# Recurrent layer of a two-layer decoder step: one visit per head with the 32-column products of three heads, states 32 projection steps behind it

## The chip, the cores and the metric

The kernel runs on one core of one Trainium2 chip, as one launch. The metric is device time in microseconds (us), median of three runs. One further execution was profiled; its trace gives each instruction's engine, start and duration. Engines: PE (TensorE matmuls), PEld (TensorE weight loads), DVE (VectorE), ACT (ScalarE), POOL (GpSimd) and SP (SyncE, which issues most DMAs).

## The reference

One inference step for 320 tokens: 256 prompt tokens, and 8 sequences with 8 new tokens each that share the weights; 16 learned meta tokens lead the prompt, so 336 columns pass through layer 0. Width 2048. Layer 0 is a gated linear recurrence (HGRN2, 16 heads of 128), layer 1 is sliding-window attention; each layer has one input projection, a gate, one output projection and a layer norm behind the residual sum. The change touches layer 0 only.

```python
def hgrn_chunk(q, logf, k, v, s0):
    b = jnp.cumsum(logf, axis=1)                       # products of the forget gates
    diff = jnp.where(causal, b[:, :, None] - b[:, None, :], -jnp.inf)
    a = jnp.sum(q[:, :, None] * jnp.exp(diff) * k[:, None, :], axis=-1)
    o = (jnp.einsum('bthk,bhkv->bthv', q * jnp.exp(b), s0)
         + jnp.einsum('btsh,bshv->bthv', a, v))
    s_new = (jnp.exp(b[:, -1])[..., None] * s0
             + jnp.einsum('bshk,bshv->bhkv', k * jnp.exp(b[:, -1][:, None] - b), v))
    return o, s_new

def hgrn_branch(xin, w_in, lb, norm_w, w_out, s0, n_lead, chunk):
    q, fx, i_in, g = jnp.split(jnp.einsum('btd,de->bte', xin, w_in), 4, axis=-1)
    f = lb + (1.0 - lb) * jax.nn.sigmoid(heads(fx))
    q, logf, k, v = heads(q), jnp.log(f), 1.0 - f, heads(i_in)
    ...                                                # chunks one after the other, state carried on
    o = o * lax.rsqrt(jnp.mean(jnp.square(o), axis=-1, keepdims=True) + RMS_EPS) * norm_w
    o = o.reshape(bsz, t, HGRN_WIDTH) * jax.nn.silu(g)
    return jnp.einsum('bte,ed->btd', o, w_out), s
```

Outputs are the tokens and the new recurrent states: one state of 128 x 128 per head for the prompt (`st_p`) and eight for the samples (`st_s`).

## The kernel before

**The stream.** All projections are one stream on TensorE. For each head there are four weight tiles of 128 output columns, in the order f (forget), q, i (values), g (gate); each takes 16 steps of k. A step of k is three matmuls of 128 x 336 (L225 to L227): the weight and the input are each split in a high and a low part, low times high, high times low and high times high. Weights come as `raw` by DMA (L148, SP), four k at a time; ACT casts the high part `whi` (L159) and DVE subtracts for the low part `wlo` (L170), seven chunks ahead of use. The chunk with the last four k of a tile is taken first, so a tile starts with its `wlo_..._3`. Behind each step the stream lets side generators emit some of a head's own work; `yield n` in such a generator means "n steps later". The order of emission is the order of the queues: each engine takes its instructions strictly in that order.

**A head's own work.** `head_chain(h)` builds the products over time by doubling: levels of 1, 2, 4 and 8 tokens give `lv_a`, products with 32 output columns (L514); VectorE picks from them by mask (L521, L522). Levels of 16 to 64 give `lv_b` (L514, L591, L596). kx and qx are the scaled keys and queries of a level. Then follow the transposes `pk`, `pv` (L603, L606), the state products `psp` (prompt, L660) and `pss` (samples, L664), the output `po` (32-column products L692 to L699, then 128-column ones L701 to L704), its squares on ACT (L709), the mean `ss` (L710, DVE), its power on POOL (L711), the scaling `osc` (L714, DVE), the transposes `pt` (L720) and the gated output `og`, `oh`, `ol` (L725, L278, L279), which is the input of the output projection. `ns` is the samples' new state: s0 times fs on POOL (L675), plus pss on DVE (L679), stored by SP (L680).

**Where it stands.** Two visits per head interrupt the projections. Visit a, four steps into tile g of head h: lv_a of head h, psp and pss of h-1, pt of h-2. Visit b, 14 steps later, in tile f of the next head: lv_b, pk and pv of head h, po of h-1. PSUM buffers are few: `pj` and `pm` banks rotate between projections and head products, `lv` holds lv_a and lv_b, and pt is written into the old lv_b.

**The end of the layer.** The output projection has 16 tiles z0 to z15. Three of them (z0 to z2) run side by side, k outermost, while the last heads finish, since each k of theirs needs one head's output. From z3 on they go one after the other. A `z_chain` behind each tile adds the residual (L790, L791), scales (L792, L793 and L794), and writes the next layer's input xh (L795) and xl (L804). The z buffers are opened in memory that the recurrence's pool has given back, so z0 waits until the last ns has been stored.

Of the kernel before, what the change touches and what calls it, by code (L numbers as in the profile page):

```python
# [21 lines left out]
F32 = mybir.dt.float32  # L22
# [217 lines left out]
def hybrid_trunk(tc, x_prompt, x_sample, state_hgrn, cache_k, cache_v, meta, w_in0, lb_logits, norm_w, w_out0,  # L240
# [7 lines left out]
    with es:  # L248
# [97 lines left out]
        for nm, w in (("f", 384), ("qp", 448), ("iT", 384), ("at", 3 * 132), ("a32", 96), ("sq0", 288),  # L346
                      ("sq1", 288), ("qi0", 177), ("qi1", 177), ("w64", 72)):
            one[nm] = hp1.tile([P, w], F32, tag=nm, name=nm)
            nc.gpsimd.memset(one[nm], 1.0 if nm == "w64" else 0.0)
        kx, qx = [], []  # L350
        for q in range(1, 4):
            for l, nm, w in ((kx, "kx", 384), (qx, "qx", 448)):
                l.append(hp1.tile([P, w], F32, tag=f"{nm}{q}", name=f"{nm}{q}"))
                nc.gpsimd.memset(l[-1], 0.0)
# [90 lines left out]
        def epi_g(h):  # L445
            def epi(ps):
                d = head_state(h)
                sg = hp.tile([P, T], F32, tag="sg", name=f"sg{h}")
# [3 lines left out]
                nc.sync.dma_start(s0, state_hgrn[0, :, h].rearrange("b k v -> k b v"))  # L452
                d["s0"] = s0

                def chain():
                    yield 2
                    nc.vector.tensor_tensor(sg, sg, ps, op=ALU.mult)  # L457
                    ready["g", h] = True
                st.spawn(chain())
            return epi  # L460
# [5 lines left out]
        def update(k, q, m, tot, n, k2=None, q2=None, nq=None):  # L466
# [5 lines left out]
            w = min(n, 448 - (m - 1)) // (2 * m) * 2 * m  # L472
# [4 lines left out]
            if q2 is not None and not nq:  # L477
                nc.scalar.copy(halves(q2, m - 1, m, w, True), halves(q, m - 1, m, w, True))
# [17 lines left out]
        tails = {}  # L496

        def adv(h):
            if h in tails:
                next(tails[h], None)  # L500

        def head_chain(h):
            d = head_state(h)
            kr, qp, a32, sq, qi = d["kr"], d["qp"], d["a32"], d["sq"], d["qi"]
            at = d["at"].rearrange("p (b w) -> p b w", b=3)
            kk = [kr] + kx
            qq = [qp] + qx

            def level(pl, o, li, wide=True):
                k, q = kk[min(li, 3)], qq[min(li, 3)]  # L510
                for blk in range(3):
                    for j in range(4 if blk < 2 else 3 if wide else 1):
                        c = blk * 128 + j * 32
                        nc.tensor.matmul(pl[32 * j:32 * j + 32, o + blk * 32:o + blk * 32 + 32], k[:, c:c + 32],  # L514
                                         q[:, c:c + 32], start=True, stop=True, tile_position=(0, 32 * j),
                                         skip_group_check=True)

            def pick(pl, o, li, wide=True):
                m0 = li * 96
                r = 96 if wide else 32  # L520
                nc.vector.copy_predicated(a32[:, 0:64], mk[:, m0:m0 + 64], pl[:, o:o + 64])  # L521
                nc.vector.copy_predicated(a32[0:r, 64:96], mk[0:r, m0 + 64:m0 + 96], pl[0:r, o + 64:o + 96])  # L522

            tot = {1: d["f"]}
            yield 3
            for li in range(3):
                m = 1 << li
                update(kk[li], qq[li], m, tot[m], 352, kk[li + 1], qq[li + 1])
                tot[2 * m] = total(h, m, tot[m], 352)
                yield 4  # L530

            k8, q8 = kk[3], qq[3]
            fs = hp.tile([P, 8], F32, tag="fs", name=f"fs{h}")
            t8 = tot[8]
            nc.gpsimd.tensor_copy(fs, t8[:, 36:44])
            w64 = d["w64"]
            nc.gpsimd.tensor_copy(w64[:, 0:64].rearrange("p (b t) -> p b t", t=8)[:, :, 7], fs)

            for s in range(3):
                n = 3 if s < 2 else 2  # L540
                nc.gpsimd.tensor_tensor(sq[:, 0:96 * n].rearrange("p (j w) -> p j w", w=96)[:, :, 40 * s:40 * s + 8],
                                        q8[:, 288:288 + 24 * n].rearrange("p (j w) -> p j w", w=24)[:, :, 8 * s:8 * s + 8],
                                        w64[:, 0:24 * n].rearrange("p (j w) -> p j w", w=24)[:, :, 8 * s:8 * s + 8],
                                        op=ALU.mult)
            yield 4

            pa = lv.tile([P, 512], F32, tag="lv", name=f"lv{h}_a")
            for li in range(4):
                level(pa, 96 * li, li)
            adv(h - 1)  # L550
            adv(h - 2)
            yield 1
            update(k8, q8, 8, t8, 272)
            tot[16] = hp.tile([P, 17], F32, tag="tot16", name=f"tot{h}_16")
            t8v = t8[:, 0:34].rearrange("p (b two) -> p b two", two=2)
            nc.vector.tensor_tensor(tot[16], t8v[:, :, 0], t8v[:, :, 1], op=ALU.mult)
            for li in range(4):
                pick(pa, 96 * li, li)
            adv(h - 1)
            yield 2  # L560
            t16 = tot[16][:, 16:17]
            update(k8, q8, 16, tot[16], 256, kk[1], qq[1])
            tot[32] = total(h, 16, tot[16], 256)
            nc.vector.tensor_scalar(qq[1][:, 271:272], q8[:, 271:272], t16, None, op0=ALU.mult)
            yield 3
            adv(h - 2)
            update(kk[1], qq[1], 32, tot[32], 256, kk[2], qq[2])
            nc.scalar.copy(qi[:, 144:161], qq[1][:, 255:272])
            t64 = total(h, 32, tot[32], 256)
            t128 = hp.tile([P, 2], F32, tag="t128", name=f"t128_{h}")  # L570
            nc.vector.tensor_tensor(t128[:, 0:1], t64[:, 2:3], t64[:, 3:4], op=ALU.mult)
            yield 3
            adv(h - 1)
            k64 = kk[2]
            nc.vector.tensor_tensor(halves(kr, 0, 64, 256), halves(k64, 0, 64, 256),
                                    t64.rearrange("p (b two) -> p b two", two=2)[:, :, 1:2].to_broadcast([P, 2, 64]),
                                    op=ALU.mult)
            nc.scalar.copy(halves(kr, 0, 64, 256, True), halves(k64, 0, 64, 256, True))
            nc.vector.tensor_scalar(qi[:, 64:128], qq[2][:, 191:255], t64[:, 2:3], None, op0=ALU.mult)
            nc.scalar.copy(qi[:, 0:64], qq[2][:, 127:191])  # L580
            yield 5
            while ("i", h) not in ready:
                yield 0

            pb = lv.tile([P, 512], F32, tag="lv", name=f"lv{h}_b")
            d["pb"] = pb
            level(pb, 0, 4, wide=False)
# [11 lines left out]
            adv(h - 1)  # L599
            iT = d["iT"]  # L600
            pk = pm(f"pk{h}")
            for j in range(3):
                nc.tensor.transpose(pk[:, j * P:(j + 1) * P], (kr if j < 2 else k8)[:, j * P:(j + 1) * P], ident)  # L603
            pv = pm(f"pv{h}")
            for j in range(3):
                nc.tensor.transpose(pv[:, j * P:(j + 1) * P], iT[:, j * P:(j + 1) * P], ident)  # L606
            yield 1
            pick(pb, 0, 4, wide=False)
            for a in range(2):
                nc.scalar.copy(at[64 * a:64 * a + 32, 0:2, 64 * a + 32:64 * a + 64],  # L610
                               pb[64 * a:64 * a + 32, 96:160].rearrange("p (b w) -> p b w", b=2))
            nc.scalar.copy(at[0:64, 0:2, 64:128], pb[0:64, 160:288].rearrange("p (b w) -> p b w", b=2))
            for blk in range(3):
                o = 1 if blk < 2 else 0
                nc.vector.copy_predicated(
                    at[:, blk, o:o + 128].rearrange("p (j w) -> p j w", w=32),
                    mk[:, 480 + blk * 128:608 + blk * 128].rearrange("p (j w) -> p j w", w=32),
                    a32[:, blk * 32:blk * 32 + 32].unsqueeze(1).to_broadcast([P, 4, 32]))
            V = hp1.tile([P, 3, P], F32, tag="V", name=f"V{h}")
            K = hp1.tile([P, 2, P], F32, tag="K", name=f"K{h}")  # L620
# [27 lines left out]
            for w, us in ((1, (h - 1,)), (3, (h - 1,)), (6, (h,)), (2, (h - 1, h)), (1, (h - 1, h)), (4, (h,)), (3, (h,)),  # L648
                          (2, (h,)), (4, (h,)), (1, (h,))):
                yield w  # L650
                for u in us:
                    adv(u)
# [849 lines left out]
```

## Time and profile before

| | |
|---|---|
| time, median of 3 runs | 1155.39 us (1155.0 to 1156.29) |
| time of the profiled execution | 1155.55 us |
| its span, first to last instruction | 1153.5 us |
| mean granted TensorE clock | 0.997 |
| PE / DVE / ACT / POOL busy | 1138.6 / 795.3 / 619.8 / 238.8 us |
| DMA traffic | 173.39 MB, mean 150 GB/s |
| TensorE's longest waits | 1.2 us (pj_z for DVE sg), 1.1, 1.0, 0.7, 0.6 |

A row of a timeline gives the start, the duration, the engine, line and operation, the output and inputs, the count, and in brackets the idle time ahead of it with what ended it. Matmul durations overlap, so costs on PE are differences of starts. A product of plain f32 counts as two matmuls in the trace and as one in the order lists below.

### The profile page before, as it was taken

To read this page: it belongs to the slowest core of one execution; us is meant where nothing else is said; L and a number is where in the kernel's file an instruction comes from. 1 tells how busy PE (TensorE), PEld (TensorE's weight loads), DVE (VectorE), ACT (ScalarE), POOL (GpSimd) and SP (SyncE) were. 2 spreads that over 40 slices of the span, in tenths; PEclk is the share of its full clock that TensorE was granted. 3 is DMA by queue.
4 is the path that set the end of the run, shared out by engine and by line. 5 is a ranking of instruction groups with operands and counts; after the bars stand their busy time and mean duration, and the time that the engine had idled before them with its cause. 6 is when DMAs were issued, how large, how long until landed. Compare 5 with 4: busy or idle time off the path is not lost.

```text
span 1153.5 us, 26363 instructions
## 1 busy us (share of the span) xinstructions
PE 1138.6 (99%) x10151; PEld 1105.6 (96%) x10151; DVE 795.3 (69%) x2094; ACT 619.8 (54%) x1771; POOL 238.8 (21%) x343
## 2 busy tenths in 40 slices
PE   9999999999999999999999999999999999999996
PEld 9999999999999999999999999998999999999995
DVE  4766566666576565666678777577878767787657
ACT  4664555545555545555445445566666655555540
POOL 2121221212212112212134332100000011145510
PEclk9999999999999999999999999999999999999998
DMA  9654565445554545654455545653533535545572
GB/s 255 190 148 132 165 178 144 133 141 168 165 155 144 149 132 165 182 145 134 135 169 146 147 143 140 199 143 106 137 106 106 147 101 166 146 134 159 155 211 91
DMA packets 322877, 173.39 MB, mean 150 GB/s; under 512 B 19104, under 2 KB 317536, under 8 KB 322720
## 3 DMA queue, kind: packets, MB, share of 16 engines
q1 hardware_dynamic: 320656, 166.98, 51.4%
q0 software_dynamic: 1344, 4.20, 1.3%
q8 instruction: 80, 1.31, 0.5%
q10 hardware_dynamic: 752, 0.52, 0.1%
q14 instruction: 45, 0.37, 0.1%
HBM read 158.88 MB, written 14.42 MB: 150 GB/s over the span
## 4 chain that ended last, share of the span: by engine, by line
PE 94%; DVE 3%; ACT 1%; DMA 0%; issue 0%; SPq 0%; POOL 0%; DVEq 0%
PE pj_g L225 7%; PE pj_g L226 7%; PE pj_g L227 7%; PE pj_q L225 6%; PE pj_q L226 6%; PE pj_q L227 6%; PE pj_f L225 3%; PE pj_i L225 3%; PE pj_f L226 3%; PE pj_f L227 3%; PE pj_i L227 3%; PE pj_i L226 3%; PE pj_z L225 3%; PE pj_z L227 3%; PE pj_z L226 3%; PE pj_y L225 2%
## 5 line engine op out<-in xcount | busy, mean ns | idle before, releaser
L225 PE MATMUL pj_g<-xh,wlo_g 128*128 128x336 f32 (+1 forms) x512 | 163.1, 319 | 0.0
L225 PE MATMUL pj_q<-xh,wlo_q 128*128 128x336 f32 (+1 forms) x512 | 163.0, 318 | 0.0
L226 PE MATMUL pj_g<-xl,whi_g 128*128 128x336 f32 (+1 forms) x512 | 160.8, 314 | 0.0
L226 PE MATMUL pj_q<-xl,whi_q 128*128 128x336 f32 (+1 forms) x512 | 160.8, 314 | 0.0
L227 PE MATMUL pj_g<-xh,whi_g 128*128 128x336 f32 (+1 forms) x512 | 160.6, 314 | 0.0
L227 PE MATMUL pj_q<-xh,whi_q 128*128 128x336 f32 (+1 forms) x512 | 160.4, 313 | 0.0
L225 PEld LDWEIGHTS pj_q<-xh,wlo_q 128*128 128x128 f32 x512 | 96.8, 189 | 0.7
L225 PEld LDWEIGHTS pj_g<-xh,wlo_g 128*128 128x128 f32 x512 | 96.8, 189 | 0.3
L226 PEld LDWEIGHTS pj_g<-xl,whi_g 128*128 128x128 f32 x512 | 97.0, 189 | 0.0
L226 PEld LDWEIGHTS pj_q<-xl,whi_q 128*128 128x128 f32 x512 | 96.9, 189 | 0.0
L227 PEld LDWEIGHTS pj_q<-xh,whi_q 128*128 128x128 f32 x512 | 96.7, 189 | 0.0
L227 PEld LDWEIGHTS pj_g<-xh,whi_g 128*128 128x128 f32 x512 | 96.6, 189 | 0.0
L170 DVE TENSOR_TENSOR wlo_g<-raw_g,whi_g 128x512 fp32r<-128x512 f32 x128 | 91.8, 752 | 0.1
L159 ACT CAST whi_g<-raw_g 128x512 fp32r<-128x512 f32 x128 | 76.4, 622 | 21.6 <-DMA raw_g<-in_hgrn_w_in_dram 13.0
L170 DVE TENSOR_TENSOR wlo_q<-raw_q,whi_q 128x512 fp32r<-128x512 f32 x128 | 85.2, 685 | 2.5 <-ACT whi_q L159 2.5
L636 POOL TENSOR_TENSOR vm<-Vs,cst 96x512 fp32r<-96x512 f32 x32 | 33.7, 1055 | 252.4 <-DVE Vs L633 251.3
L225 PE MATMUL pj_f<-xh,wlo_f 128*128 128x336 f32 x256 | 83.2, 325 | 0.0
L225 PE MATMUL pj_z<-oh,wlo_z 128*128 128x336 f32 x256 | 81.5, 318 | 1.2 <-DVE sg L457 1.2
L225 PE MATMUL pj_i<-xh,wlo_i 128*128 128x336 f32 x256 | 81.5, 318 | 0.0
L226 PE MATMUL pj_f<-xl,whi_f 128*128 128x336 f32 x256 | 81.3, 318 | 0.0
L227 PE MATMUL pj_z<-oh,whi_z 128*128 128x336 f32 x256 | 81.3, 317 | 0.0
L227 PE MATMUL pj_f<-xh,whi_f 128*128 128x336 f32 x256 | 81.1, 317 | 0.0
(404 smaller groups left out, 3217.4 us busy)
## 6 DMA issues: line engine op xcount, KB each, us to landing
raw_z<-in_hgrn_w_out_dram SPq DMA_DIRECT2D x32, 512.0 KB
raw_q<-in_swa_w_in_dram SPq DMA_DIRECT2D x32, 512.0 KB
raw_g<-in_swa_w_in_dram SPq DMA_DIRECT2D x32, 512.0 KB
raw_f<-in_hgrn_w_in_dram SPq DMA_DIRECT2D x30, 512.0 KB
raw_q<-in_hgrn_w_in_dram SPq DMA_DIRECT2D x30, 512.0 KB
raw_i<-in_hgrn_w_in_dram SPq DMA_DIRECT2D x30, 512.0 KB
raw_g<-in_hgrn_w_in_dram SPq DMA_DIRECT2D x30, 512.0 KB
raw_y<-in_swa_w_out_dram SPq DMA_DIRECT2D x24, 512.0 KB
```

The source lines that it names most:

```text
L159: e.nc.scalar.copy(hi, t["raw", kc])
L170: e.nc.vector.tensor_tensor(lo, t.pop(("raw", kc)), hi.bitcast(F32), op=ALU.subtract)
L225: nc.tensor.matmul(ps, lo[:, kk, :], xh, start=first, stop=False)
L226: nc.tensor.matmul(ps, hi[:, kk, :], xl, start=False, stop=False)
L227: nc.tensor.matmul(ps, hi[:, kk, :], xh, start=False, stop=last)
L636: nc.gpsimd.tensor_tensor(vm[0:96, 4 * u:4 * u + 4, :], Vs[:, u, :].bitcast(F32).unsqueeze(1).to_broadcast([96, 4, P]), cst[0:96, 0:4].uns ...
```

## The change

Per head, one visit takes the place of two. Four steps into the last tile of head h (now i; the tile order becomes f, q, g, i) stand lv_a of head h, the wide levels of h-1, the output po of h-2, and the transposes pk and pv of h-1, all by `visit0(h)`. pt of h-2 stands alone nine steps behind it, psp and pss of h-1 alone 32 steps behind it. In the order of TensorE this reads, before, from visit a of head 7 (names end in the head's number; the projections between are left out here):

```order
L514 MATMUL lv7_a_4167<-qp_147,kr7_3981 32x32 x11
L514 MATMUL lv7_a_4167<-qx1_167,kx1_165 32x32 x11
L514 MATMUL lv7_a_4167<-qx2_171,kx2_169 32x32 x11
L514 MATMUL lv7_a_4167<-qx3_175,kx3_173 32x32 x11
L660 MATMUL psp6_4212<-V6_3892,K6_3893 128x128 x2
L660 MATMUL psp6_4212<-V6_3892,K2_177 128x128
L664 MATMUL pss6_0_4216<-vm6_3899,Ks6_3897 128x512
L664 MATMUL pss6_1_4218<-vm6_3899,Ks6_3897 128x512
L720 MATMUL lv6_b_3835<-ident_110,osc5_3940 128x128 x3
```

and now, from the visit of head 8:

```order
L524 MATMUL lv8_a_4597<-qx3_0_175,kx3_0_173 32x32 x11
L524 MATMUL lv7_b_4642<-qx3_1_187,kx3_1_185 32x32 x9
L536 MATMUL lv7_b_4642<-qx1_1_179,kx1_1_177 32x32 x2
L541 MATMUL lv7_b_4642<-qx2_1_183,kx2_1_181 32x64 x2
L536 MATMUL lv7_b_4642<-qx1_1_179,kx1_1_177 32x32 x2
L541 MATMUL lv7_b_4642<-qx2_1_183,kx2_1_181 32x64 x2
L558 MATMUL po6_4660<-S6_4430,qi0_159 32x128
L562 MATMUL po6_4660<-s0_6_3730,sq0_155 32x128 x8
L558 MATMUL po6_4660<-S6_4430,qi0_159 32x128
L565 MATMUL po6_4660<-V6_4220,at_151 32x128 x4
```

The 128-column products of po, pk and pv follow as before; psp, pss and pt have left the visit.

On VectorE, behind the products of po, before (head 6):

```order
L615 COPY_PREDICATED at_151<-mk_133,a32_153 128x128 x3
L633 TENSOR_TENSOR Ks7_4401<-pk7_4375,Ks7_4401 32x128
L633 TENSOR_TENSOR Vs7_4402<-pv7_4379,Vs7_4402 32x128
L633 TENSOR_TENSOR Ks7_4401<-pk7_4375,Ks7_4401 32x128
L633 TENSOR_TENSOR Vs7_4402<-pv7_4379,Vs7_4402 32x128
L457 TENSOR_TENSOR sg7_4326<-sg7_4326,pj_g7_4152 128x336
L710 TENSOR_SCALAR ss6_4429<-ss6_4429 128x3
L170 TENSOR_TENSOR wlo_q8_3_4439<-raw_q8_2_4078,whi_q8_3_4330 128x512
L714 TENSOR_TENSOR osc6_4444<-po6_4357,ss6_4429 128x384
```

and now (head 5; L576 and L577 are the picks, L760 is osc), from the last of four pairs of picks, which stand behind ss:

```order
L576 COPY_PREDICATED a32_153<-mk_133,lv7_a_4093 128x64
L577 COPY_PREDICATED a32_153<-mk_133,lv7_a_4093 96x32
L170 TENSOR_TENSOR wlo_f8_3_4215<-raw_f8_2_3919,whi_f8_3_4075 128x512
L473 TENSOR_TENSOR kx3_1_185<-kx3_1_185,tot7_8_4051 128x17x8
L477 TENSOR_TENSOR qx3_1_187<-qx3_1_187,tot7_8_4051 128x17x8
L629 TENSOR_TENSOR tot7_16_4232<-tot7_8_4051 128x17
L760 TENSOR_TENSOR osc5_4198<-po5_4156,ss5_4197 128x384
```

The picks of the new head's lv_a, a weight conversion and the level of 8 now stand between ss and osc; the copies of Ks and Vs and the product with sg have gone to other places.

At the end of the layer, VectorE before, from the low part of head 15's gated output on (the ns15 adds stand eleven rows ahead of it):

```order
L279 TENSOR_TENSOR ol15_657<-og15_8638,oh15_641 128x336
L170 TENSOR_TENSOR wlo_z3_1_8646<-raw_z3_0_8333,whi_z3_1_8606 128x512
L170 TENSOR_TENSOR wlo_z3_2_8662<-raw_z3_2_8461,whi_z3_2_8626 128x512
L170 TENSOR_TENSOR wlo_z3_3_8680<-raw_z3_2_8461,whi_z3_3_8654 128x512
L790 SCALAR_TENSOR_TENSOR z0_8703<-xh0_78,pj_z0_8364 128x336
L791 SCALAR_TENSOR_TENSOR z0_8703<-xl0_94,z0_8703 128x336
L804 TENSOR_TENSOR xl0_94<-zg0_8704,xh0_78 128x338
L170 TENSOR_TENSOR wlo_z4_0_8717<-raw_z4_0_8499,whi_z4_0_8672 128x512
```

and now:

```order
L279 TENSOR_TENSOR ol15_669<-og15_8696,oh15_653 128x336
L170 TENSOR_TENSOR wlo_z4_0_8704<-raw_z4_0_8424,whi_z4_0_8661 128x512
L744 TENSOR_TENSOR ns15_8679<-ns15_8679,pss15_0_8670 128x512
L744 TENSOR_TENSOR ns15_8679<-ns15_8679,pss15_1_8672 128x512
L170 TENSOR_TENSOR wlo_z4_1_8724<-raw_z4_0_8424,whi_z4_1_8684 128x512
L170 TENSOR_TENSOR wlo_z4_2_8742<-raw_z4_2_8529,whi_z4_2_8714 128x512
L838 SCALAR_TENSOR_TENSOR z0_8767<-xh0_78,pj_z0_8350 128x336
L839 SCALAR_TENSOR_TENSOR z0_8767<-xl0_94,z0_8767 128x336
L852 TENSOR_TENSOR xl0_94<-zg0_8768,xh0_78 128x338
L170 TENSOR_TENSOR wlo_z4_3_8781<-raw_z4_2_8529,whi_z4_3_8734 128x512
```

The ns15 adds (L744) have moved from ahead of og15 to behind it, and z0 (L838) stands ahead of the last conversion of z4, which tile z4 needs first. On SP the store of ns15 now follows raw_z6_0 and st_p15.

Further parts: kx and qx exist twice, by the parity of the head (six more memsets by POOL at the start); s0 is loaded four steps behind the visit instead of with g; squares are written into osc, which saves `junk`; ns takes the buffer of vm; sp has two buffers and sg three. st_p and st_s go out together, three steps behind the ns adds. Heads 14 and 15 are quick: their psp stands 7 and 6 steps behind their visits, pss 14 steps behind psp. The output projection runs four tiles side by side instead of three, the fourth in an lv bank, and the z chains come 1, 5, 9 and 13 steps late instead of 1, 7 and 13.

The diff's core (moved functions are left out where only their place changed):

```diff
-                s0 = hp.tile([P, 8, P], F32, tag="s0", name=f"s0_{h}")
-                nc.sync.dma_start(s0, state_hgrn[0, :, h].rearrange("b k v -> k b v"))
...
+        def visit0(h, pa=None):
+            if pa is not None:
+                for li in range(4):
+                    level(hd[h], pa, 96 * li, li)
+            if 1 <= h <= H:
+                wide_levels(h - 1)
+            if h >= 2:
+                output(h - 2)
+            if 1 <= h <= H:
+                d = hd[h - 1]
+                d["pk"], d["pv"] = pm(f"pk{h - 1}"), pm(f"pv{h - 1}")
...
+            if h >= 2:
+                st.spawn(normed(h - 2), 1)
...
+        def head_chain(h):
+            kk = d["kk"] = [kr] + kx[h % 2]
...
+            visit0(h, pa)
+            yield 1
+            if h:
+                attended(h - 1)
+                st.spawn(states(h - 1), 2)
+                yield 1
+            for li in range(4):
+                pick(d, pa, 96 * li, li)
+            yield 2
+            update(k8, q8, 8, t8, 272)
...
+            nc.sync.dma_start(s0, state_hgrn[0, :, h].rearrange("b k v -> k b v"))
...
+        def states(h):
+            quick = h >= H - 2
...
+            if quick:
+                yield 4
+                behind_chunks()
+                yield 1
+                evicted()
+                yield 2
+            else:
+                yield 13
+            while h and ("ns", h - 1) not in ready:
+                yield 0
...
+                yield (8 if quick else 11) if u else (3 if quick else 5)
+            if not quick:
+                behind_chunks()
...
+            yield 1
+            if not quick:
+                evicted()
+            ns = hp1.tile([P, 8, P], F32, tag="vm", name=f"ns{h}")
+            nc.gpsimd.tensor_tensor(ns, s0, fs.unsqueeze(2).to_broadcast([P, 8, P]), op=ALU.mult)
+            yield 6
+            for u in range(2):
...
+                nc.vector.tensor_tensor(nu, nu, pss[u], op=ALU.add)
+            ready["ns", h] = True
+            yield 3
+            nc.sync.dma_start(st_p[0, 0, h], d["sp"])
+            nc.sync.dma_start(st_s[0, :, h].rearrange("b k v -> k b v"), ns)
+
+        def normed(h):
+            osc = hp1.tile([P, 3, P], F32, tag="osc", name=f"osc{h}")
             for j in range(3):
+                nc.scalar.activation(osc[:, j, :], po[:, j * P:(j + 1) * P], AF.Square, accum_out=ss[:, j:j + 1])
             nc.vector.tensor_scalar(ss[:, 0:3], ss[:, 0:3], 1.0 / 128, RMS_EPS, op0=ALU.mult, op1=ALU.add)
             nc.gpsimd.tensor_tensor(ss[:, 0:3], ss[:, 0:3], mhalf[:, 0:3], op=ALU.pow)
+            yield 4
             nc.vector.tensor_tensor(osc, po[:, 0:384].rearrange("p (j v) -> p j v", j=3),
                                     ss[:, 0:3].unsqueeze(2).to_broadcast([P, 3, P]), op=ALU.mult)
+            yield 4
+            while h >= H - 3 and h < H - 1 and ("Ks", h + 1) not in ready:
+                yield 0
-            pt = hd[h + 1]["pb"] if h < H - 1 else pm(f"pt{h}")
+            pt = pm(f"pt{h}")
...
-            for nm, off, epi in (("f", 1, epi_f), ("q", 0, epi_q), ("i", 2, epi_i), ("g", 3, epi_g)):
+            for nm, off, epi in (("f", 1, epi_f), ("q", 0, epi_q), ("g", 3, epi_g), ("i", 2, epi_i)):
...
-            yield 1 + 6 * j if j < 3 else 1
+            yield 1 + 4 * j if j < 4 else 1
...
-        st.add(zt[:3], kouter=True)
-        st.add(zt[3:])
+        zt[3]["bank"] = lv, "lv"
+        st.add(zt[:4], kouter=True)
+        st.add(zt[4:])
```

More of the change, by code (lines that the diff above doesn't have):

```diff
@@ L488, in total @@
             return o
[L496 to L587, printed above, removed]
@@ L598, in head_chain @@
                                      stop=True, tile_position=(0, 32 * a), skip_group_check=True)
[L599 to L618, printed above, removed]
```

246 lines of the change are left out of this document (167 added, 79 removed).

## The prediction

> **What bounds the kernel now.** I read the busy shares first, then the chain of waits and the list of TensorE's waits, then the timeline of each engine around one head's products and around the end of the layer. From the page:
>
> ```profile
> PE 1138.6 (99%) x10151; PEld 1105.6 (96%) x10151; DVE 795.3 (69%) x2094; ACT 619.8 (54%) x1771; POOL 238.8 (21%) x343
> ...
> PEclk9999999999999999999999999999999999999998
> ...
> PE 94%; DVE 3%; ACT 1%; DMA 0%; issue 0%; SPq 0%; POOL 0%; DVEq 0%
> ```
>
> TensorE is busy 99% at the full granted clock and carries 94% of the chain. So time is gained only where TensorE does its work in less time or stops waiting, and every new wait on it counts in full. TensorE's timeline for one head, with both visits of before (a visit is the head's own products between two projections):
>
> ```profile
> 280.60 0.32 PE L227 MATMUL pj_g<-xh,whi_g 128*128 128x336 f32 x1
> 280.85 0.36 PE L514 MATMUL lv_a<-qp,kr 128*32 128x32 f32 x19
> 281.02 0.22 PE L514 MATMUL lv_a<-qx,kx 128*32 128x32 f32 x1
> ...
> 281.06 0.82 PE L514 MATMUL lv_a<-qx,kx 128*32 128x32 f32 x65
> 281.81 0.94 PE L660 MATMUL psp<-V,K 128*128 128x128 f32 x6
> ...
> 283.54 0.32 PE L226 MATMUL pj_g<-xl,whi_g 128*128 128x336 f32 x1
> ...
> 289.69 0.32 PE L227 MATMUL pj_f<-xh,whi_f 128*128 128x336 f32 x1
> ...
> 293.02 0.32 PE L226 MATMUL pj_f<-xl,whi_f 128*128 128x336 f32 x1
> ```
>
> and at the end of the layer, where the last heads' parts stand alone among the output projections:
>
> ```profile
> 578.65 0.42 PE L225 MATMUL pj_z<-oh,wlo_z 128*128 128x336 f32 x1 [1.25 <-DVE sg L457]
> ...
> 580.92 0.32 PE L227 MATMUL pj_z<-oh,whi_z 128*128 128x336 f32 x1
> ...
> 582.36 0.31 PE L226 MATMUL pj_z<-ol,whi_z 128*128 128x336 f32 x1
> ...
> 582.97 0.33 PE L227 MATMUL pj_z<-oh,whi_z 128*128 128x336 f32 x1
> ...
> 583.62 0.32 PE L226 MATMUL pj_z<-ol,whi_z 128*128 128x336 f32 x1
> ...
> 585.61 0.32 PE L227 MATMUL pj_z<-oh,whi_z 128*128 128x336 f32 x1
> ...
> 587.81 0.32 PE L226 MATMUL pj_z<-ol,whi_z 128*128 128x336 f32 x1
> ```
>
> Starts tell the cost, since durations overlap. The projections from 583.62 to 585.61 are 13 starts apart: 0.153 us each. From the last L227 ahead of a visit to the first L226 behind it lie two such steps (0.31) and the visit: visit a (lv_a, psp, pss, pt) costs 2.94 - 0.31 = 2.63 us, visit b (wide levels, po, pk, pv) 3.33 - 0.31 = 3.02. Alone, psp with pss cost 1.44 - 0.31 = 1.13, pt 0.65 - 0.31 = 0.34, po 2.20 - 0.31 = 1.89.
>
> **The change part by part.**
>
> *1. Visits.* The new visit is visit b with the 88 matmuls of lv_a ahead of it. These end at 281.88; one lasts about 0.2, so the last starts at 281.68, 0.83 behind the first; with the change of shape behind them it is 0.96 (to 281.81). In the joint visit the next products have 32 columns too, so I take 0.84: 3.86. psp with pss (1.13) and pt (0.34) now stand alone: 5.33 per head against 5.65, so -0.32, at worst (0.96) -0.20. Over 14 heads this is -4.5. At the layer's ends the first visits lose a split (-0.3), and the two last heads' psp and pss, now apart, gain one shape change each (about 0.1, as 0.96 against 0.84, so +0.2). **-4.6 us**, from -2.8 to -5.
>
> *2. The wait of 1.25 us* at 578.65: bank pj_z2 was that of g15, read late by L457 behind visit b's copies. With g ahead of i the tile ends 16 steps sooner. **-1.25**.
>
> *3. pt(h-2) waits for osc.* In the changed kernel pt comes nine steps behind the visit that made its po: 27 projections. In between lie copies on ACT, squares, the power on POOL and the scaling osc, in queues that now hold other work. Rows of before for each:
>
> ```profile
> 292.41 0.42 ACT L610 COPY at<-lv_b 32x64 f32<-32x64 f32 x2 [2.33 <-PE po L704]
> ...
> 293.07 0.48 ACT L621 COPY V<-pv 128x384 f32<-128x384 f32 x1
> ...
> 587.93 0.28 ACT L709 ACTIVATE junk<-po 128x128 f32<-128x128 f32 x1 [0.77 <-PE po L704]
> ...
> 589.13 0.17 DVE L710 TENSOR_SCALAR ss<-ss 128x3 f32<-128x3 f32 x1
> ...
> 579.28 1.22 POOL L711 TENSOR_TENSOR ss<-ss,mhalf 128x3 f32<-128x3 f32 x1
> ...
> 281.90 0.30 DVE L475 TENSOR_TENSOR kx<-kx,tot 128x136 f32<-128x136 f32 x1 [5.35 <-PE lv_a L514]
> ...
> 282.41 0.22 DVE L521 COPY_PREDICATED a<-mk,lv_a 128x64 f32<-128x64 uint8 x1
> ...
> 283.44 0.34 DVE L669 SCALAR_TENSOR_TENSOR S<-S,t,psp 128x128 f32<-128x128 f32 x1
> ...
> 590.26 0.56 DVE L714 TENSOR_TENSOR osc<-po,ss 128x384 f32<-128x384 f32 x1 [0.96 <-POOL ss L711]
> ```
>
> Count from ACT's first copy behind po (292.41) as 0. Three copies take 0.66 (293.07), the squares 1.20 (587.93 to 589.13): ss stands at 1.86 and ends at 2.0, POOL's power (1.22) at 3.3. VectorE cannot take osc then: behind ss stand eight picks (282.41 to 283.44: 1.03), one weight conversion (0.60, three in 1.89 at 594.39 below), kx, qx and tot16 (281.90 to 282.41: 0.51): 4.1, and osc ends at 4.65. TensorE wants it at 293.02 - 0.15 + 27 x 0.153 - 292.41 = 4.6, its weight load 0.15 sooner. So pt comes 0.1 to 0.2 late, and all projections of that tile stand behind it. I take 0.2 for 13 heads: **+2.6**, from 0 (osc without the picks ahead of it) to +5 (0.4, one more conversion half in the way).
>
> *4. The quick heads.* psp14 takes the bank of po13, and psp15 that of po14; osc is the last to read either. They come seven and six steps behind the visit instead of nine. By the count of part 3 psp14's weights are wanted at 4.45 - 6 x 0.153 = 3.5, and osc13 ends at 4.65: 1.1 late. For psp15 it is 3.07, and osc14 has no picks of a next head and one conversion ahead of it, so POOL's power decides: 3.3 and 0.56 of its own (590.26) are 3.9, 0.8 to 0.9 late. **+2.0**, from 0 to +2.5.
>
> *5. z0 waits for the last state's store.* z0 is written where ns15 lay, so it waits for the landing of ns15's store, in both kernels. Before, POOL shows that landing, and z0 came later:
>
> ```profile
> 573.51 2.70 SPq L452 DMA_DIRECT2D s<-in_state_hgrn_dram  x1
> ...
> 588.93 0.57 SPq L673 DMA_DIRECT2D out_dram<-sp  x1
> 589.60 0.39 SPq L680 DMA_DIRECT2D out_dram<-ns  x1
> ...
> 581.24 2.21 POOL L675 TENSOR_TENSOR ns<-s,fs 128x1024 f32<-128x1024 f32 x1 [0.74 <-DMA s<-in_state_hgrn_dram]
> ...
> 594.88 0.24 POOL L793 COPY zg<-tv 128x1 f32<-128x1 f32 x1 [4.65 <-DMA out_dram<-ns]
> ...
> 586.58 1.28 DVE L679 TENSOR_TENSOR ns<-ns,pss 128x512 f32<-128x512 f32 x2
> ...
> 592.35 0.89 DVE L725 SCALAR_TENSOR_TENSOR og<-pt,tv,sg 128x255 f32<-128x255 f32 x4 [0.94 <-PE pt L720]
> ...
> 594.39 1.89 DVE L170 TENSOR_TENSOR wlo_z<-raw_z,whi_z 128x512 fp32r<-128x512 f32 x3
> 597.44 0.50 DVE L790 SCALAR_TENSOR_TENSOR z<-xh,pj_z 128x336 f32<-128x336 f32 x1 [1.16 <-PE pj_z L227]
> ...
> 600.25 1.89 DVE L170 TENSOR_TENSOR wlo_z<-raw_z,whi_z 128x512 fp32r<-128x512 f32 x3
> ...
> 591.83 0.49 PE L720 MATMUL pt<-ident,osc 128*128 128x128 f32 x3
> ```
>
> The store was issued at 589.60 and had landed at 594.88: 5.28. In the changed kernel ns15 is finished behind og15. Count from pt15 (591.83 here): og starts at 0.52 and its group ends at 2.56 (594.39), one conversion 3.16, the two ns adds (1.28 as shown at 586.58, 1.2 between starts) 4.35, a second conversion 5.0, for which SP's next weight load waits; behind that load (about 0.5) and st_p (0.67) the store goes out at 6.2 and lands at 11.5. z0, xl0 and what lies between take 2.81 (597.44 to 600.25), and only then comes wlo_z4_3, which TensorE needs first for tile z4: 14.95. TensorE is ready for it 69 projections behind pt15, at 0.34 + 10.56 = 10.9. It idles 4.1. Behind the waiting z0 on VectorE stand that conversion and those of z5, on ACT zg0, xh0 and the casts of z5. z5 then wants four conversions and two z chains, 2.4 + 5.6 = 8.0 us of VectorE in the 7.4 us (48 projections) that z4 lasts: 0.6 more. **+4.7**, from 0 (the wait ends before it is wanted) to +7 (the s0 load took up to 7.7 from 573.51 to 581.24, 2.4 more than 5.28).
>
> A page bears on the length of this gap. The Trainium skill (TensorE: Matmul & The Clock Gate, the clock gate) says that the array's clock falls to half after an idle window of about 3.4 us, in windows that run freely. By it the sum would be an estimated 1.7 us or more higher if a window fell inside the gap; no wait of TensorE's here is longer than 1.25 us, so no row shows it.
>
> *At no cost:* six more memsets (POOL is 21% busy and ahead of the first head idle), the doubled kx and qx, squares into osc, s0's load issued some steps later (used 28 steps on), st_p held back to st_s (nothing reads it; the buffer is doubled). The cover for the shared vm and ns buffer is 35 steps, 16 us, against a store of 5.28; if it went, pss would be late by the difference.
>
> **Sum.** -4.6 - 1.25 + 2.6 + 2.0 + 4.7 = +3.45 on the profiled execution's 1155.55: 1159.0. That execution stands 0.16 above the median of 1155.39, so the forecast for a median is 1158.8.
>
> **The rivals.**
> - *The store does not hold z0* (not slower): if it lands by 7.4 behind pt15 (10.9 - 2.81 - 0.65), nothing is left of part 5, and up to 10.2 the whole stays below 1157.7. For it: with the two ns adds ahead of og15 on VectorE, as at 586.58 before, it would go out 1.8 sooner, and every step of the count is one row's. Against: the og group, the conversions and 5.28 of transfer stand one behind the other in the order of their queues. 1158.8 - 4.7 = 1154.1.
> - *osc is in time.* Parts 3 and 4 rest on 0.1 to 0.2 us; 0.3 less on VectorE and both go: 1158.8 - 4.6 = 1154.2. For it: the lateness per head is no longer than a single pick, so a small error of the count decides. Against: picks, conversion and kx stand ahead of osc in VectorE's queue whatever POOL does.
> - *Neither wait comes*: 1158.8 - 4.7 - 4.6 = 1149.5, faster.
> - *The gap costs clock as well.* If TensorE ran at half speed for as long as it idled (4.1), half of that is lost: +2.05, 1160.9. Against: the granted clock shows no such stretch, but no such gap either.
> - *The change does not do what it says*: lv_a costs its 0.96 in the joint visit too and the parts alone cost as much as shown. The visits bring -2.8 instead of -4.6: 1160.6.
>
> **How the numbers follow.** About 0.2% (2.3 us) is what a measurement of this kernel can tell from no change. Chances: both waits 0.40 (its own range 1156.7 to 1161.3), no store wait 0.15, osc in time 0.17, neither 0.20, the clock 0.05, dear visits 0.03. Faster, below 1153.1, is "neither" and the lower edge of the two halves: 0.25. Within 0.2% are the rest of the halves: 0.28. Slower 0.47. The range from 1151.0 to 1163.0 leaves out the lower half of "neither" and the longest gaps.
>
> **What would show it.** Visits: one group of 32-column products a head, 3.86 us, with projections between it and two lone parts, pt and psp with pss. Part 2: no wait on sg. Parts 3 and 4: in the list of waits, pt and psp waiting for DVE osc, 13 times about 0.2 and twice about 1. Part 5: one TensorE wait of about 4 us on wlo_z at z4's start, a DVE z0 waiting for DMA out_dram<-ns. A list without the last, or pt waiting for something other than osc, proves me wrong.

## The result and the profile after

The changed kernel takes 1161.9 us (median of four runs, 1161.75 to 1162.99) against 1155.84 for the kernel before on the same chip: ratio 1.0055, 95% interval 1.0038 to 1.0073. It is 6.1 us slower. The forecast was 3.45 us slower. From the page of the changed kernel:

```profile
PE 1136.6 (98%) x10151; PEld 1104.2 (95%) x10151; DVE 829.5 (72%) x2094; ACT 615.7 (53%) x1771; POOL 258.6 (22%) x349
...
PEclk9999999999999999999998999999999999999998
...
PE 88%; DVE 6%; ACT 2%; DMA 2%; issue 1%; POOL 0%; SPq 0%; DVEq 0%; ACTq 0%; POOLq 0%
```

TensorE is busy 2.0 us less, and yet the span is 6.5 us longer: its share of the chain fell from 94 to 88%, and one slice of the granted clock reads 8 where there was a 9 before. Its list of waits (us in total, times, longest) names the places:

```profile
PE pj_z L225 <- DVE wlo_z L170: 5.4, 2, 4.6
PE psp L693 <- DVE osc L760: 2.0, 2, 1.5
...
PE pss L734 <- POOL vm L723: 0.8, 2, 0.5
...
PE po L565 <- issue: 0.2, 1, 0.2
```

No pt waits, and the wait for sg has gone. TensorE's timeline around the visit of one steady head and its pt:

```profile
240.71 0.31 PE L227 MATMUL pj_i<-xh,whi_i 128*128 128x336 f32 x1
...
244.85 0.32 PE L226 MATMUL pj_i<-xl,whi_i 128*128 128x336 f32 x1
...
248.69 0.32 PE L227 MATMUL pj_i<-xh,whi_i 128*128 128x336 f32 x1
...
249.33 0.31 PE L226 MATMUL pj_i<-xl,whi_i 128*128 128x336 f32 x1
```

As in the prediction, two steps (0.31) come off: the visit costs 4.14 - 0.31 = 3.83 (3.86 was worked out), pt 0.33. So the saving per head is there. What took more than it gave stands at the layer's end, here from the timelines of POOL, SP, DVE and PE:

```profile
591.89 2.08 POOL L723 TENSOR_TENSOR vm<-Vs,cst 96x512 fp32r<-96x512 f32 x2 [9.50 <-DMA out_dram<-ns]
...
602.12 0.57 SPq L747 DMA_DIRECT2D out_dram<-sp  x1
602.74 0.43 SPq L748 DMA_DIRECT2D out_dram<-ns  x1
...
600.94 1.29 DVE L170 TENSOR_TENSOR wlo_z<-raw_z,whi_z 128x512 fp32r<-128x512 f32 x2
607.95 0.51 DVE L838 SCALAR_TENSOR_TENSOR z<-xh,pj_z 128x336 f32<-128x336 f32 x1 [5.72 <-DMA out_dram<-ns]
...
610.76 1.29 DVE L170 TENSOR_TENSOR wlo_z<-raw_z,whi_z 128x512 fp32r<-128x512 f32 x2
...
606.60 0.31 PE L227 MATMUL pj_z<-oh,whi_z 128*128 128x336 f32 x1
611.50 0.65 PE L225 MATMUL pj_z<-oh,wlo_z 128*128 128x336 f32 x1 [4.59 <-DVE wlo_z L170]
611.94 0.48 PE L226 MATMUL pj_z<-ol,whi_z 128*128 128x336 f32 x1
...
615.58 0.37 PE L227 MATMUL pj_z<-oh,whi_z 128*128 128x336 f32 x1
615.79 0.32 PE L225 MATMUL pj_z<-oh,wlo_z 128*128 128x336 f32 x1
```

ns15's store goes out at 602.74 and has landed at 607.95 (5.21); only then does z0 run, and behind it, at 610.76, the conversion that z4 needs. TensorE stands still from 606.75 to 611.5. Then its matmuls start 0.28 us apart, 13 of them, before they are back at 0.153. The stretches of the gap and behind it (us, PE busy, PEld, DVE, ACT, POOL, granted clock, DMA share, GB/s) show why:

```profile
607.00:611.50 4.50, 0.00 (x1) 0.01 (x1) 2.18 (x5) 2.09 (x4) 1.34 (x6) 0.71 0.02 6
611.50:615.60 4.10, 4.10 (x15) 4.10 (x16) 3.88 (x8) 2.46 (x5) 0.78 (x1) 0.50 0.45 130
```

TensorE worked at half the clock for 4.1 us. The 0.71 of the first row shows that the clock had fallen inside the gap already. The account, from differences of starts on TensorE in the two profiled executions:

| part | forecast | measured |
|---|---|---|
| visits and lone parts, without waits (90.85 to 86.16) | -4.6 | -4.7 |
| short gaps inside six visits | 0 | +1.7 |
| wait for sg | -1.25 | -1.4 |
| pt waits for osc | +2.6 | 0 |
| psp14, psp15 wait for osc | +2.0 | +2.4 |
| pss15 waits for vm15 | 0 | +1.1 |
| gap at z4, and z6 later | +4.7 | +4.75 + 1.0 |
| half clock behind the gap | 0 (a rival, +2.05) | +1.9 |
| start of the program | 0 | -0.5 |
| sum | +3.45 | +6.2 |

The two profiled executions took 1161.75 and 1155.55, 6.2 apart.

### The profile page after: what moved, and what is told of

Same layout as the page of the kernel before. It is cut to its first block, busy times and chain, and to the rows that moved or that the text cites. A ratio compares the mean times of both kernels' runs of the same rounds, so it can differ in the third digit from the quotient of the medians.

```text
span 1160.0 us, 26288 instructions
## 1 busy us (share of the span) xinstructions
PE 1136.6 (98%) x10151; PEld 1104.2 (95%) x10151; DVE 829.5 (72%) x2094; ACT 615.7 (53%) x1771; POOL 258.6 (22%) x349
## 3 DMA queue, kind: packets, MB, share of 16 engines
q8 instruction: 80, 1.31, 0.5%
## 4 chain that ended last, share of the span: by engine, by line
PE 88%; DVE 6%; ACT 2%; DMA 2%; issue 1%; POOL 0%; SPq 0%; DVEq 0%; ACTq 0%; POOLq 0%
PE pj_g L225 7%; PE pj_g L226 7%; PE pj_g L227 7%; PE pj_q L225 6%; PE pj_q L226 6%; PE pj_q L227 6%; PE pj_f L225 3%; PE pj_f L227 3%; PE pj_f L226 3%; PE pj_i L225 3%; PE pj_i L226 3%; PE pj_i L227 3%; PE pj_y L225 2%; PE pj_y L227 2%; PE pj_y L226 2%; PE pj_z L225 2%
## 5 line engine op out<-in xcount | busy, mean ns | idle before, releaser
L226 PE MATMUL pj_q<-xl,whi_q 128*128 128x336 f32 (+1 forms) x512 | 160.7, 314 | 0.0
L226 PE MATMUL pj_g<-xl,whi_g 128*128 128x336 f32 (+1 forms) x512 | 160.6, 314 | 0.0
L170 DVE TENSOR_TENSOR wlo_g<-raw_g,whi_g 128x512 fp32r<-128x512 f32 x128 | 121.4, 982 | 0.4
L226 PEld LDWEIGHTS pj_q<-xl,whi_q 128*128 128x128 f32 x512 | 96.8, 189 | 0.6
L226 PEld LDWEIGHTS pj_g<-xl,whi_g 128*128 128x128 f32 x512 | 96.8, 189 | 0.0
L226 PE MATMUL pj_z<-ol,whi_z 128*128 128x336 f32 x256 | 81.8, 320 | 0.0
L226 PE MATMUL pj_f<-xl,whi_f 128*128 128x336 f32 x256 | 81.0, 316 | 0.1
L226 PE MATMUL pj_i<-xl,whi_i 128*128 128x336 f32 x256 | 80.9, 316 | 0.0
```

The lines of the kernel that those rows point to most:

```text
L170: e.nc.vector.tensor_tensor(lo, t.pop(("raw", kc)), hi.bitcast(F32), op=ALU.subtract)
L226: nc.tensor.matmul(ps, hi[:, kk, :], xl, start=False, stop=False)
```

## The experiments

**1. The stores off z0's memory.** The recurrence's pool is given back as a whole, so z0 waits for everything that still reads from it. Here vm, ns and sp move to a pool that stays open (ns and sp by the same edit as vm; the mask staging buffer takes a weight buffer to make room).

```diff
+            nsp.append(oes.enter_context(tc.tile_pool(name="nsp", bufs=1, side="right")))
-            vm = hp1.tile([P, 8, P], F32R, tag="vm", name=f"vm{h}")
+            vm = nsp[0].tile([P, 8, P], F32R, tag="vm", name=f"vm{h}")
...
```

> The changed kernel with vm, ns and sp in a pool that stays open past the recurrence (the mask staging buffer moves to a weight buffer to make room), so that z0 no longer waits for the landing of ns15's store; nothing else moves. Theory (store holds z0, z0 holds the conversion that z4 needs, and the clock falls in the gap): the wait of 4.6 us at z4 goes, no matmul starts 0.28 us apart behind it, and of the 1.0 us wait at z5 little stays: 4.75 + 2.0 + 1.0 = 7.8 us less than the changed kernel, 1154.1 (1153 to 1155.5). Rival (z0 is held by VectorE's own queue or by its bank, whatever the store does): a wait of over 2 us stays there, 1158 to 1162.

Measured: 1156.16, ratio to before 1.001 (1.000 to 1.0019). From the timelines of DVE and SP, and the waits:

```profile
602.39 0.50 DVE L841 SCALAR_TENSOR_TENSOR z<-xh,pj_z 128x336 f32<-128x336 f32 x1
...
602.98 0.43 SPq L751 DMA_DIRECT2D out_dram<-ns  x1
...
PE pj_z L225 <- DVE wlo_z L170: 1.7, 1, 1.7
```

z0 now runs before the store is even issued, the gap at z4 and the slow matmuls are gone, and the time falls by 5.7 us: the store's chain is shown as the cause. Of the 7.8 expected some 2 did not come. Most of that is the wait further on: it was to go and grew from 1.0 to 1.7. It stands at z6, not z5 as I had written. TensorE reaches z6 sooner, while VectorE's work is no faster: from z0 to TensorE's start on z6 21.3 us pass (602.39 to 623.72), in the changed kernel 21.4 (607.95 to 629.33).

**2. The last two heads' stores by GpSimd.**

```diff
-            yield 3
-            nc.sync.dma_start(st_p[0, 0, h], d["sp"])
-            nc.sync.dma_start(st_s[0, :, h].rearrange("b k v -> k b v"), ns)
+            if not quick:
+                yield 3
+            dq = nc.gpsimd if quick else nc.sync
+            dq.dma_start(st_p[0, 0, h], d["sp"])
+            dq.dma_start(st_s[0, :, h].rearrange("b k v -> k b v"), ns)
```

> The changed kernel, but the state transfers of the two last heads are issued by GpSimd right behind the ns adds, not by SyncE three steps later behind its weight loads. Theory: st_s14 lands near 583 instead of 591.9, so vm15 and pss15 no longer wait (0.46 us less there), ns15's store goes out 1.7 us sooner and the wait at z4 shrinks to about 3.4 or less. If the clock needs an idle stretch of about that length, the half-speed matmuls go as well: 1.7 + 2.0 less, 1158.2. If the clock falls after any such gap: 1.7 less, 1160.2. Rival (a store issued by GpSimd takes longer to land or the queue of SyncE was not what held it): no gain, 1161.9.

Measured: 1159.92, ratio 1.0039 (1.0024 to 1.0054). POOL's timeline, TensorE's waits and the stretch behind the gap:

```profile
576.70 0.92 POOL L750 DMA_DIRECT2D out_dram<-ns  x1 [3.38 <-DVE wlo_z L170]
580.61 1.25 POOL L760 TENSOR_TENSOR ss<-ss,mhalf 128x3 f32<-128x3 f32 x1 [3.00 <-DMA out_dram<-ns]
...
PE pj_z L225 <- DVE wlo_z L170: 4.5, 2, 3.3
...
608.90:612.20 3.30, 3.30 (x14) 3.30 (x13) 3.08 (x7) 2.21 (x5) 0.52 (x1) 0.51 0.56 161
```

st_s14 has landed by 580.61, not 591.89, and pss no longer waits: it was SyncE's queue, where the store stood behind a weight load that waited for its buffer. The gap at z4 shrinks to 3.3 us and the clock falls all the same. psp waits 0.4 longer than in the changed kernel (2.4 us in all). Of the two figures expected, the one with the clock falling (1160.2) is the nearer to the one measured.

**3. The squares into a scratch tile again.**

```diff
+            junk = hp1.tile([P, P], F32, tag="junk", name=f"junk{h}")
...
-                nc.scalar.activation(osc[:, j, :], po[:, j * P:(j + 1) * P], AF.Square, accum_out=ss[:, j:j + 1])
+                nc.scalar.activation(junk, po[:, j * P:(j + 1) * P], AF.Square, accum_out=ss[:, j:j + 1])
```

> The changed kernel with the squares written to one shared scratch tile as before the change, not to osc. In the changed trace the three squares start 0.25 us apart, before 0.40. Theory (the squares into osc are what let osc be in time for pt, with 0.2 us to spare): squares 0.40 apart again, osc 0.3 to 0.45 later, pt waits 0.1 to 0.25 in some 13 heads and psp14 0.3 more: 1163 to 1165.5. Rival (VectorE's queue sets osc, the squares have slack, or the spacing has another cause): 1161.9.

Measured: 1165.24, ratio 1.0085 (1.007 to 1.010). ACT and DVE of the changed kernel in a steady head, then of this one:

```profile
244.24 0.42 ACT L586 COPY at<-lv_b 32x64 f32<-32x64 f32 x2 [3.55 <-PE po L570]
...
244.83 0.27 ACT L756 ACTIVATE osc<-po 128x128 f32<-128x128 f32 x1
...
245.09 0.26 ACT L756 ACTIVATE osc<-po 128x128 f32<-128x128 f32 x1
...
245.73 0.17 DVE L757 TENSOR_SCALAR ss<-ss 128x3 f32<-128x3 f32 x1
...
247.94 0.55 DVE L760 TENSOR_TENSOR osc<-po,ss 128x384 f32<-128x384 f32 x1
```

```profile
244.43 0.42 ACT L586 COPY at<-lv_b 32x64 f32<-32x64 f32 x2 [3.55 <-PE po L570]
...
245.02 0.27 ACT L757 ACTIVATE junk<-po 128x128 f32<-128x128 f32 x1
...
245.41 0.28 ACT L757 ACTIVATE junk<-po 128x128 f32<-128x128 f32 x1
...
248.42 0.54 DVE L761 TENSOR_TENSOR osc<-po,ss 128x384 f32<-128x384 f32 x1
```

Squares into three places start 0.26 apart, into one place 0.40. osc starts 3.70 and 3.99 behind ACT's first copy. With 0.29 more, pt costs 0.42 to 0.45 instead of 0.33 in each steady head (0.1 times 13: 1.4 us), psp waits 0.8 longer, and the clock fell once more, behind psp15's wait (11 matmuls at 0.28: 1.4). Together 3.6, near the 3.3 measured.

**4. pt two steps sooner.** `yield 4` ahead of pt becomes `yield 2`.

> The changed kernel with pt seven steps behind the visit instead of nine. Theory (osc ends 0.2 us ahead of pt's weight load in the steady heads): two steps are 0.92 us, so pt waits 0.7 us for osc in 13 or 14 heads, 9 to 10 us more: 1171. Rival (osc has a step or two in reserve): 1161.9 to 1163.

Measured: 1171.55, ratio 1.0139 (1.0123 to 1.0154). From the waits:

```profile
PE pt L768 <- DVE osc L760: 7.5, 14, 0.5
```

The time grew by 9.65 us, 0.69 for each of the 14 waits, where pt came 0.92 sooner. So osc has some 0.2 us to spare in the changed kernel, and each tenth beyond is paid in every head.

**5. The tile order alone, in the kernel before.**

```diff
-            for nm, off, epi in (("f", 1, epi_f), ("q", 0, epi_q), ("i", 2, epi_i), ("g", 3, epi_g)):
+            for nm, off, epi in (("f", 1, epi_f), ("q", 0, epi_q), ("g", 3, epi_g), ("i", 2, epi_i)):
...
```

> The kernel before with one part of the change: tiles f, q, g, i instead of f, q, i, g (and three sg buffers, without which it can't run). Theory (the wait of 1.25 us at pj_z2 comes from g15's bank being read late): that wait goes and nothing else changes, 1154.3. Rival (the last tile's bank is read late whichever tile it is, or a wait of the same length comes up elsewhere, since iT is now written two steps ahead of pv): 1155.6 or more.

Measured: 1155.09, ratio 0.9995 (0.9986 to 1.0004): no difference by the time. The trace shows the wait for sg gone and a shorter one in its place:

```profile
580.58 0.47 PE L664 MATMUL pss<-vm,Ks 96*128 96x512 f32 x1 [0.62 <-DVE osc L714]
```

**6. psp of the last heads later**, on top of the first experiment.

```diff
-            if quick:
-                yield 4
-                behind_chunks()
-                yield 1
-                evicted()
-                yield 2
-            else:
-                yield 13
+            yield 7 if quick else 13
...
-                yield (8 if quick else 11) if u else (3 if quick else 5)
+                if quick and not u:
+                    yield 1
+                    behind_chunks()
+                    yield 1
+                    evicted()
+                    yield 1
+                else:
+                    yield (8 if quick else 11) if u else 5
```

> The first experiment's kernel (stores off z0's memory) with psp of heads 14 and 15 four steps later, between the two halves of vm. Theory (psp waits 0.55 and 1.6 us for osc, which reads the old bank): four steps are 1.84 us, so both waits go, 1156.2 - 2.1 = 1154.1. Rival (pss15, which waits for vm15 and so for the landing of st_s14, comes to wait by what psp no longer does): 1155.5 to 1156.2, with a pss wait of 1 us or more in place of 0.5.

Measured: 1156.14, ratio 1.0001 (0.9992 to 1.001): nothing gained. Neither psp nor pss waits any longer, but pt13 does:

```profile
568.51 0.52 PE L771 MATMUL pt<-ident,osc 128*128 128x128 f32 x3 [1.88 <-DVE sp L704]
```

The releaser is sp, which reads the moved psp14 and so comes later. My reading was that pt13 takes the bank of pk14, which Ks reads, and that Ks now stands behind S and sp on VectorE. The trace does not bear that out in full: the second half of Ks runs from 568.39 to 568.68, and pt13 starts at 568.51, behind sp and before that end. Either way the wait was passed on, to a place that neither theory had named.

**7. z chains six steps apart**, on top of the first.

```diff
-            yield 1 + 4 * j if j < 4 else 1
+            yield 1 + 6 * j if j < 4 else 5 if j == 4 else 1
```

> The first experiment's kernel with the z chains of the four joint tiles six steps apart instead of four (and z4's four steps later, to keep their order). Theory (the wait of 1.7 us at z5 is VectorE's queue: the chains of z1 to z3 stand ahead of the conversion that z5 needs first): with z3's chain behind that conversion the wait shrinks to 0.5 or less, 1154.7. Rival (the weights of z5 arrive late, or the bank of z1 is what holds it): the wait stays, 1156.2.

Measured: 1155.81, ratio 1.0001 (0.9991 to 1.001). The wait falls from 1.7 to 1.2 us (`pj_z` for `wlo_z`), between what theory and rival had said. By the time alone nothing is decided.

**8. All remedies together.**

> All remedies in one: the changed kernel with the stores off z0's memory, the last two heads' stores issued by GpSimd, psp of heads 14 and 15 four steps later, z chains six steps apart. If the changed kernel's losses are what the traces show (7.8 for the store's chain, 2.1 for psp, 0.5 to 0.8 for pss, and the 1.7 at z5 that is left after the first), this gives 1156.2 - 2.1 - 0.7 - 1.4 = 1152.0, 0.3% under the kernel before. If the losses replace one another it stays above 1154.

Measured: 1155.13, ratio 0.999 (0.9982 to 0.9999), 3 us above the expectation. pt13 waits as in the sixth, and in the profiled execution the clock fell behind that wait. The stretches of its gap and behind it, then those of the sixth kernel with nearly the same gap, 2.05 for 2.06 us (there PE alone is listed; the last section comes back to the pair):

```profile
565.70:567.90 2.20, 0.31 (x3) 0.28 (x3) 2.07 (x6) 1.51 (x5) 0.73 (x1) 1.00 0.89 248
568.10:571.40 3.30, 3.30 (x14) 3.30 (x13) 2.70 (x9) 1.40 (x3) 1.54 (x1) 0.51 0.58 154
```

```profile
566.00:568.50 2.50, 0.63 (x5) 1.00 0.84 224
568.50:572.50 4.00, 3.99 (x26) 1.00 0.69 194
```

**9. The same, with Ks ahead of S and sp.**

```diff
...
+                if quick and u:
+                    behind_chunks()
+                    yield 1
+                    evicted()
+                    yield 7
+                else:
+                    yield 11 if u else 3 if quick else 5
...
```

> The kernel with all remedies again, but with psp of heads 14 and 15 behind both halves of vm, so that Ks and Vs no longer stand behind S and sp on VectorE. Theory (the 1.9 us that pt13 waited in the two kernels with psp moved is that queue, the old wait passed on): no wait of pt, psp or pss is over 0.5 us; the layer keeps its shorter visits and loses only the 1.1 us at z6: 1155.1 - 1.9 (and - 1.5 in runs in which the clock fell there) = 1152.5 (1151 to 1153.5), faster than the kernel before by 0.2 to 0.4%. Rival (the wait is passed on again, to po15 or pt14): 1154 or more.

Measured: **1152.52, ratio 0.9972 (0.9963 to 0.9982)**, faster than both kernels. Its longest waits, without those that the kernel before has too:

```profile
PE pt L772 <- DVE Ks L717: 1.4, 1, 1.4
...
PE pj_z L225 <- DVE wlo_z L170: 1.1, 1, 1.1
```

The time came as expected, but in part for another reason. pt13 still waits 1.4, so only 0.5 of the 1.9 went. The clock, which had fallen in the profile of the eighth, did not fall here.

**10. pt13 four steps later.** Ahead of pt, `if h == H - 3: yield 4`.

> The ninth kernel with pt13 four steps (1.84 us) later. In the ninth kernel's trace pt13 waited 1.4 us for the second half of Ks on VectorE, the last reader of the bank it takes. Theory: that wait goes: 1152.5 - 1.4 = 1151.1. Rival (og13 and the layer's last input then come late and the output projection waits for oh13, or pss14 waits): 1152.5 or more.

Measured: 1152.34, ratio 0.997 (0.9959 to 0.9981), the same as the ninth. The wait moved to pt and psp of the later heads, which neither theory nor rival had named:

```profile
PE pt L774 <- DVE Ks L717: 0.9, 1, 0.9
PE psp L696 <- DVE osc L764: 0.6, 1, 0.6
```

In each of the four kernels in which psp or pt had been moved (6, 8, 9 and 10), between 1.4 and 1.9 us of waiting was left at the end of the recurrence. That the two last heads' copies on ACT and VectorE are the limit there is my reading; no run took work off them.

## Why the prediction was right, and where it was off

**Part 1, visits: right.** 3.83 against 3.86 for the steady visit, -4.7 against -4.6 in all. Not seen were short gaps inside six of the fourteen full visits (0.05 to 0.5 each, 1.7 in all), of which the trace names what it can as "issue". They come back in every kernel with the joint visit, and in nine of these ten the largest stands in the same head, near 380 us. The instruction loads in the traces (queue q8 of the page, 80 loads, 1.31 MB) point at a cause. In all 13 visits of the ten profiles in which such a load begins 0.2 to 0.8 us behind the visit's start, the visit is 0.2 to 0.85 us longer than 3.83. In the 84 in which it begins 1.7 us or more behind it, with none shortly ahead, the visit is at most 0.08 longer. No run moved a load against a visit, so the cause stays open.

**Part 2, sg: right** in the trace (experiment 5 too, where another wait of 0.6 us took its place).

**Part 3, pt: the term that failed**, +2.6 forecast, 0 measured. The order of the queue was right and osc was the releaser (experiment 4), but three squares were priced at 1.20 from rows that write one scratch tile. Into osc they took 0.76 (from 244.83 to ACT's next copy at 245.59), VectorE began its queue at 1.49 behind ACT's first copy and not at 1.86, and osc ended at 4.25, not 4.65. I had listed "squares into osc" under no cost and kept the old price.

**Part 4: right in cause; that the size came so near (2.4 for 2.0) is luck.** psp14 lost 0.7 us for 1.1 forecast, since osc was early as in part 3, and psp15 lost 1.7 for 0.8 to 0.9. There ACT's copies behind po14 stood behind a cast whose weights had not landed:

```profile
578.80 0.62 ACT L159 CAST whi_z<-raw_z 128x512 fp32r<-128x512 f32 x1 [3.29 <-DMA raw_z<-in_hgrn_w_out_dram]
579.43 0.42 ACT L586 COPY at<-lv_b 32x64 f32<-32x64 f32 x2
```

The first copy began 0.58 behind the visit's first L226 (578.85); in the steady head it began 0.61 ahead of it (244.24 and 244.85). My count had no such cast.

**"At no cost" failed at one place:** the cover of 35 steps for the buffer shared by vm and ns holds for steady heads, not for the quick ones. There GpSimd stood idle for 9.5 us until st_s14 had landed. The first half of Vs15, which vm15 reads, was ready at 586.33, so vm15 was 5.6 us late, and pss15 lost 1.1 (experiment 2 takes it away).

**Part 5: right** in place, releaser and size: 4.75 for 4.1, and 1.0 for 0.6 behind it, though one tile later. The 0.65 too little is one term: og15 began 1.35 behind pt15 (595.77 to 597.12) and not 0.52, because the conversion ahead of it on VectorE took 1.91 us and not 0.6 (the last section shows beside what).

**The clock** was a rival with a chance of 0.05, and it happened. That its price came so near, 1.9 against the 2.05 worked out, is luck: the rival let TensorE run slow for as long as it had idled, and the traces show slow stretches of 3.41 us or twice that (last section), 3.41 behind a gap of 2.06 as behind one of 3.97. With a gap of 4 us forecast at 0.40, the chance was too low: no row of before had a gap over 1.25, so the rows could not speak against it. Here the rule of the Trainium skill (TensorE: Matmul & The Clock Gate, the clock gate), an idle window of about 3.4 us in free-running windows, was the better guide: by it the estimate was 1.7 or more. Its condition was not met, though: no whole window lay in the gap, and the clock fell all the same.

The overestimate in part 3 (2.6) and the misses in clock, pss and visit gaps (4.7) went opposite ways. That the total came out nearer than its parts is luck.

## What to carry to other kernels

Moving a transfer later is free only until its buffer, or the pool it lies in, is given back: follow the landing to whoever takes that memory next, and look what stands ahead of the store in its queue. A step that comes nearer to its producer must be costed with the rows of the form it will have (where it writes, what is ahead of it), because a tenth of a microsecond per head decides. And a wait that is moved is not removed: after each remedy look for the next bank in the rotation.

## What the runs showed of the hardware

- **A gap on TensorE costs clock as well, and where the gap lies decides.** Gaps here are differences of starts less one step. Every gap of 3.47 us or more (3.47, 3.97, 4.66 and 4.75, in four profiles) cost half speed on 3.2 to 4.1 us of work. Of four gaps of 2.01 to 2.07 us, two did (experiments 3 and 8) and two did not (2 and 6); none of 1.96 or less did. The clock records of the traces tell the two pairs apart. In each of the twelve profiles, changes of the clock lie a whole number of 3.413 us apart (604.16 us from the first to the second in the changed kernel: 177 times), and the slow stretches ahead of the program's end are 3.41 us long, in the changed kernel 6.83 (608.87 to 615.70). So the time can be cut into windows of that length. Here is the window of the gap in experiment 8, behind which the clock fell, and the one with the most of the gap in experiment 6, behind which it did not (columns as in the section on the result):

```profile
564.72:568.13 3.41, 1.52 (x11) 1.27 (x11) 3.25 (x8) 2.46 (x10) 1.54 (x1) 1.00 0.82 224
```

```profile
566.85:570.26 3.41, 1.75 (x13) 1.78 (x13) 3.22 (x9) 1.21 (x5) 1.62 (x2) 1.00 0.85 241
```

  In experiment 8 the whole gap lies in one window, in which TensorE idles for 1.89 us of 3.41 (1.91 in experiment 3, 1.96 in the changed kernel's first). In experiment 6 a window's edge cuts the gap, and 1.66 of it are left on the longer side; in experiment 2 the edge leaves 0.93 and 0.92. The most idle time of a window that left the clock full is 1.72 us (experiment 2, near 1118), but for one of 1.88 with TensorE's last matmul in it (experiment 8). So some 1.9 us in one window was enough. This was worked out afterwards; no run moved a gap against the windows. The page of the Trainium skill named above asks for one idle window of about 3.4 us. The length of the windows agrees, but a window need not be idle throughout.
- **VectorE's conversions slow down beside GpSimd's products.** The group of wlo_g in layer 0, before and after, then one row of DVE and the row of POOL beside it:

```profile
L170 DVE TENSOR_TENSOR wlo_g<-raw_g,whi_g 128x512 fp32r<-128x512 f32 x64 | 42.5, 699 | 0.1
```

```profile
L170 DVE TENSOR_TENSOR wlo_g<-raw_g,whi_g 128x512 fp32r<-128x512 f32 x64 | 72.0, 1160 | 0.4
...
261.60 2.01 DVE L170 TENSOR_TENSOR wlo_g<-raw_g,whi_g 128x512 fp32r<-128x512 f32 x1
...
261.17 1.90 POOL L740 TENSOR_TENSOR ns<-s,fs 128x1024 f32<-128x1024 f32 x1 [2.72 <-PE pss L734]
```

The conversion of 0.68 us took 2.01 while GpSimd formed ns; the moved states laid vm and ns beside these conversions, 30 us more of VectorE in all. The Trainium skill (SBUF — State Buffer, Terms) says that the two engines share a port and the loser waits for the whole instruction, which these rows agree with. In the heads it cost nothing, since TensorE waited for none of these conversions. At the layer's end the same slowing, of the conversion ahead of og15 beside ns15 (VectorE 595.29 for 1.91 us, GpSimd 594.76 for 1.89), delayed ns15's store and with it z0.
